# Weights and products of three attention stages by output tile, with PSUM banks owned by the phase

## The chip, the cores and the metric

The kernel runs on one core of a Trainium2 chip. A core has five engines, each with its own queue of instructions: PE (TensorE) multiplies matrices and writes the results to PSUM, DVE (VectorE) and ACT (ScalarE) work on tiles in SBUF and PSUM, POOL (GpSimd) works on SBUF, and SP issues most of the DMAs. PSUM has eight banks; one bank holds 512 fp32 numbers in each of 128 partitions. The metric is the time of one execution on the device, in microseconds (us), the median of several.

## The reference

One inference step of two layers over 288 tokens: 256 of a prompt and 32 of a sample group that has a cache of 256 past tokens. The model width is 1024, attention heads have 64 channels, the MLP is 4096 wide.

```
layer 0:  qa, ka, va, qb, kb, vb, fl = split(rmsnorm(x) @ ab_w_in)   # 8 heads A, 8 heads B
          A: attention over a band of chunks, relative bias, q and k normalised per head
          B: softmax attention with a forgetting term from log_sigmoid(fl + b)
          x += concat(A, B) @ ab_w_out
layer 1:  q, k, v = split(rmsnorm(x) @ sb_w_in)                      # 16 heads C
          C: stick-breaking attention
          x += C @ sb_w_out
each:     k_mem, v_mem = split(rmsnorm(mem) @ w_kv);  k_mem normalised
          x += cross_attention(rmsnorm(x) @ w_q, k_mem, v_mem) @ w_o  # 4 heads of 256
          x += square(relu(rmsnorm(x) @ w_up)) @ w_down
```

All is float32. The outputs are also the new keys and values of A, B, C, the memory keys and values, and log f.

## The kernel before

Everything is kept transposed: channels on the 128 partitions, the 288 tokens (`T`) along the free axis. The state `h` is 8 k-tiles of 128x288. A float32 product is made from three matmuls in a rounded format (`mm3`, lines 147 to 151): each operand is split into a high and a low part, and high times high, high times low and low times high are added in PSUM. So every weight is loaded by DMA into a raw buffer, rounded by ACT to `wh` (line 133; some by DVE, line 131), and subtracted by DVE to `wl` (line 134; in some stages by POOL).

Weights come in chunks of 256 output columns, two output tiles of 128. `load_chunk` (line 109) takes a chunk in two halves of four k-tiles, 512 KB each; four raw halves fit (`WR`), and three split halves (`WS // NQ`). The products of a chunk, 8 k-tiles x 2 output tiles x 3 = 48 matmuls, go to two PSUM banks, filled alternately by k (`gemm2` line 162, `Mix.products` line 498).

**Banks.** Two PSUM pools are opened once, at the top of `body`: `ps_g` with three banks for such products, and `ps_t` with one bank for nearly all else: transposes of values (`ps_vt`, line 402), sums of squares of heads (`ps_hn`, line 554), of memory keys (`ps_xn`) and of the memory (`ps_ms`), scores of the sample group (`ss` line 650, `zs` line 773), turned probabilities (`ps_pts`, `ps_ws`), and, in the phases ab and c, the sums of the RMS norm (`ps_rs`, line 203). Beside them each phase has a pool `s` of its own, in ab and c two buffers of two banks (`zz`, prompt scores). In x0 and x1 it has two single banks, and there are the pools `m` and `o` with one bank each.

**Phases.** `phase(kind)` (line 72) closes the last phase's pools, in SBUF and PSUM, and opens the next. There are four: ab (A, B and their output projection), x0 (cross-attention and MLP of layer 0), c (C and its output projection), x1 (the rest). At each border `norm_split` of the next part stands before the call of `phase`:

```
out_proj(i["ab_wo"], oh, ol)
xh, xl, rs = norm_split(1, 0)
phase("x0")
oh, ol = cross(0, xh, xl, rs, mk0, mh, ml)
```

**Order of the work.** A scheduler orders each engine's instructions by readiness and program order; `with ahead(n)` raises the priority of what it encloses. In the stages A, B and C, PE's order is written by hand (`manual_schedule`). A generator (`run_ab`, `run_c`) yields pieces of projection work, counted in matmuls: the q, k and v chunks of each group of four heads, the forget gate F, the memory M, N and the memory keys K. The attention code (`attend_ab`, `attend_c`) calls `fill(n)` at places where PE would otherwise wait for a softmax, and n matmuls' worth of projection is put there (`FILL_AB`, `FILL_C`). What has to follow a projection after some delay on PE (`norm_head`, `turn_v`, `mem_k_norm`) is put on a list by `later(n, fn)`; `due` runs what has come due, all at once.

**Evacuation.** When both tiles of a chunk are done, DVE reads the two banks: `t` for q and k of A and B (line 567), `vT` for values (line 530), `tmk` for memory keys (line 544), `qz` and `kT` in C (lines 724, 730), the addition to `h` in `out_proj` (line 841) and in the MLP (line 965). For q and k of A and B, ACT and DVE then form the two parts of the squares, PE sums them per head into `ps_hn` (lines 351, 352), ACT reads that bank and forms the root (`rstd_of`, lines 172 and 173), and DVE writes the normalised `qz` or `kT` (line 558).

## Time and profile before

| | |
|---|---|
| runs, us | 953.79, 955.01, 954.6; median 954.6 |
| profiled execution, us | 954.6 |
| its span, first to last instruction, us | 952.9 |
| granted TensorE clock, mean | 0.999 |
| DMA moved, MB | 160.01 |

By stretches of the span, from the table of windows (us of busy time):

| stretch | what runs | PE | DVE | ACT |
|---|---|---|---|---|
| 0 to 24 | load of `x`, first projections | 20.45 | 19.22 | 14.36 |
| 24 to 169 | stages A and B with projections and memory keys | 135.89 | 113.25 | 105.51 |
| 169 to 194 | `out_proj` of layer 0, start of cross-attention | 24.92 | 21.35 | 14.43 |
| 194 to 286 | cross-attention 0 | 92.00 | 70.66 | 49.50 |
| 286 to 491 | MLP 0, start of C's projections | 205.00 | 149.74 | 107.33 |
| 491 to 657 | stage C and its `out_proj` | 165.54 | 116.35 | 96.62 |
| 657 to 750 | cross-attention 1 | 92.51 | 76.20 | 47.98 |
| 750 to 953 | MLP 1 | 199.33 | 110.40 | 94.92 |

How to read the lines that follow. A line of a group names the source line, the engine, the operation, the tile written and the tiles read, the shapes, the count; behind the bar the busy time, the mean of one in ns, and the idle time before them with what ended it. A line of the waits names who waited, the releaser, and the total, the number of times and the longest wait in us. A line of the timeline has the start in us, the duration, and in brackets the engine's idle time before it. A line of the windows has the stretch, its length, the busy time and number of instructions of PE, its weight loads, DVE, ACT and POOL, the granted clock, the DMA share and GB/s. Matmuls overlap: one shows about 0.29 us, though they start 0.13 us apart.

### The profile page before, as it was taken

To read this page: it belongs to the slowest core of one execution; us is meant where nothing else is said; L and a number is where in the kernel's file an instruction comes from. 1 tells how busy PE (TensorE), PEld (TensorE's weight loads), DVE (VectorE), ACT (ScalarE), POOL (GpSimd) and SP (SyncE) were. 2 spreads that over 40 slices of the span, in tenths; PEclk is the share of its full clock that TensorE was granted. 3 is DMA by queue.
4 is the path that set the end of the run, shared out by engine and by line. 5 is a ranking of instruction groups with operands and counts; after the bars stand their busy time and mean duration, and the time that the engine had idled before them with its cause. 6 is when DMAs were issued, how large, how long until landed. Compare 5 with 4: busy or idle time off the path is not lost.

```text
span 952.9 us, 19195 instructions
## 1 busy us (share of the span) xinstructions
PE 935.6 (98%) x7284; PEld 909.1 (95%) x7284; DVE 677.2 (71%) x1462; ACT 530.7 (56%) x1232; POOL 161.2 (17%) x192
## 2 busy tenths in 40 slices
PE   8999899999999999999999999999999999999998
PEld 7889889999999999999999899999989999999998
DVE  8869858778687767676786757778977765555643
ACT  5868757556456635354556655654544665454531
POOL 4000000111122221122100000004434111111110
PEclk9999999999999999999999999999999999999999
DMA  7665444654554545554465444465444555545452
GB/s 240 237 201 164 153 159 161 219 174 156 166 167 157 175 157 170 162 173 161 158 205 183 146 158 136 158 221 172 148 134 145 162 171 165 167 161 171 155 177 73
DMA packets 50700, 160.01 MB, mean 168 GB/s; under 512 B 6296, under 2 KB 12968, under 8 KB 50352
## 3 DMA queue, kind: packets, MB, share of 16 engines
q1 hardware_dynamic: 46864, 148.69, 48.8%
q0 software_dynamic: 2592, 8.92, 2.4%
q10 hardware_dynamic: 1152, 1.18, 0.4%
q8 instruction: 57, 0.93, 0.4%
q14 instruction: 35, 0.29, 0.1%
HBM read 148.65 MB, written 10.12 MB: 167 GB/s over the span
## 4 chain that ended last, share of the span: by engine, by line
PE 87%; DVE 7%; ACT 3%; DMA 2%; issue 1%; SPq 0%; DVEq 0%; ACTq 0%
PE g L149 26%; PE g L150 26%; PE g L151 26%; DVE wl L134 2%; DMA raw<-in_ab_w_dram 1%; ACT wh L133 1%; PE zz L442 1%; DVE pr L664 1%; PE zz L813 1%; PE zz L768 1%; PE zz L452 1%; ACT pr L668 1%; DMA h<-in_xT_dram 0%; DVE spl L801 0%; PE sx L149 0%
## 5 line engine op out<-in xcount | busy, mean ns | idle before, releaser
L133 ACT ACTIVATE wh<-raw 128x512 fp32r<-128x512 f32 (+3 forms) x541 | 268.9, 547 | 245.6 <-PE g L150 130.8
L134 DVE TENSOR_TENSOR wl<-raw,wh 128x512 fp32r<-128x512 f32 (+3 forms) x519 | 318.0, 651 | 102.9 <-ACT wh L133 93.2
L149 PE MATMUL g<-xh,wh 128*128 128x288 f32 (+1 forms) x1032 | 304.2, 299 | 0.6 <-DVE tmk L544 0.3
L150 PE MATMUL g<-xl,wh 128*128 128x288 f32 (+1 forms) x1032 | 302.7, 296 | 1.2 <-DVE xl L186 1.1
L151 PE MATMUL g<-xh,wl 128*128 128x288 f32 (+1 forms) x1032 | 301.4, 296 | 1.3 <-DVE wl L134 1.3
L134 POOL TENSOR_TENSOR wl<-raw,wh 128x256 fp32r<-128x256 f32 (+2 forms) x105 | 123.1, 1172 | 435.0 <-ACT wh L133 331.8
L149 PEld LDWEIGHTS g<-xh,wh 128*128 128x128 f32 (+1 forms) x1032 | 191.8, 187 | 3.5 <-issue 0.9
L151 PEld LDWEIGHTS g<-xh,wl 128*128 128x128 f32 (+1 forms) x1032 | 192.2, 187 | 3.0 <-DVE wl L134 2.2
L150 PEld LDWEIGHTS g<-xl,wh 128*128 128x128 f32 (+1 forms) x1032 | 192.4, 187 | 2.7 <-DVE xl L186 2.2
L150 PE MATMUL g<-hl,wh 128*128 128x288 f32 x512 | 150.3, 295 | 0.0
L149 PE MATMUL g<-hh,wh 128*128 128x288 f32 x512 | 148.9, 295 | 0.0
L151 PE MATMUL g<-hh,wl 128*128 128x288 f32 x512 | 148.5, 294 | 0.0
L150 PEld LDWEIGHTS g<-hl,wh 128*128 128x128 f32 x512 | 96.1, 188 | 0.0
L151 PEld LDWEIGHTS g<-hh,wl 128*128 128x128 f32 x512 | 95.7, 188 | 0.0
L149 PEld LDWEIGHTS g<-hh,wh 128*128 128x128 f32 x512 | 95.3, 187 | 0.0
L150 PE MATMUL g<-ol,wh 128*128 128x288 f32 x256 | 75.1, 296 | 0.0
L149 PE MATMUL g<-oh,wh 128*128 128x288 f32 x256 | 74.0, 296 | 0.3 <-ACT oh L461 0.3
L151 PE MATMUL g<-oh,wl 128*128 128x288 f32 x256 | 73.7, 295 | 0.0
L131 DVE CAST wh<-raw 128x256 fp32r<-128x256 f32 (+2 forms) x83 | 32.5, 391 | 39.5 <-PE g L150 20.1
L965 DVE TENSOR_TENSOR h<-h,g 128x288 f32<-128x288 f32 x64 | 28.8, 451 | 29.6 <-PE g L151 29.5
L150 PEld LDWEIGHTS g<-ol,wh 128*128 128x128 f32 x256 | 48.1, 188 | 0.3 <-issue 0.2
L149 PEld LDWEIGHTS g<-oh,wh 128*128 128x128 f32 x256 | 47.5, 188 | 0.6 <-ACT oh L461 0.4
(272 smaller groups left out, 1418.3 us busy)
## 6 DMA issues: line engine op xcount, KB each, us to landing
raw<-in_w_up_dram SPq DMA_DIRECT2D x64, 512.0 KB, 3.8
raw<-in_w_down_dram SPq DMA_DIRECT2D x64, 512.0 KB, 3.8
raw<-in_w_kv_dram SPq DMA_DIRECT2D x32, 512.0 KB, 3.8
raw<-in_sb_w_dram SPq DMA_DIRECT2D x24, 512.0 KB, 4.2
raw<-in_ab_w_dram SPq DMA_DIRECT2D x22, 512.0 KB, 5.2
raw<-in_w_q_dram SPq DMA_DIRECT2D x16, 512.0 KB, 4.1
raw<-in_w_o_dram SPq DMA_DIRECT2D x16, 512.0 KB, 4.1
raw<-in_ab_wo_dram SPq DMA_DIRECT2D x8, 512.0 KB, 3.9
```

What stands on the lines that cost most here:

```text
L131: dve.tensor_copy(wh[:, r, :], src)
L133: cast = act(wh[:, r, :], src, AF.Copy).ins
L134: e.tensor_tensor(wl[:, r, :], src, wh[:, r, :].bitcast(F32), ALU.subtract)
L149: mm(out, lh, rh, start=first, stop=False)
L150: mm(out, lh, rl, start=False, stop=False)
L151: return mm(out, ll, rh, start=False, stop=last)
L442: mm(po[64 * par:64 * par + 64, kk * P:NP_], vt[:, kk, cols], pts[par][kk], start=kk == 0, stop=kk == 1)
L452: mm(po[64 * par:64 * par + 64, p * NS:(p + 1) * NS], vs[kk][:, cols], pts[kk][:, q], start=kk == 0 and p == 0, stop=kk == 2, skip_group_c ...
L664: dve.tensor_tensor_reduce(out=pr, in0=s, in1=b, scale=1.0, scalar=-3.0e38, op0=ALU.add, op1=ALU.max, accum_out=mx[:, j:j + 1])
L668: act(pr, pr, AF.Exp, bias=nm[:, j:j + 1], accum_out=sm[:, j:j + 1])
L768: mm(block(zz, e, kk), kT[r, p, kk * P:(kk + 1) * P], qz[r, p, kk * P:NP_].rearrange("p (b c) -> p b c", c=P), start=kk == 0, stop=False, ...
L965: dve.tensor_tensor(h[:, kt, :], h[:, kt, :], ps[:, 0:T], ALU.add)
```

## The change

**By output tile.** In A, B, C, their memory keys and their two output projections, a chunk is now worked one output tile of 128 columns after the other: 24 matmuls into one bank, then 24 into the next. `load_tiles` takes the place of `load_chunk` there: it loads the two raw halves, then splits the weights of the first tile from both halves, then those of the second; a buffer of split weights now holds all eight k-tiles of one output tile. `products` calls `take(d, ...)`, the evacuation, as soon as tile d is done, and yields 6 at a time. The first projection `qA0` keeps its old weights, sliced by tile.

**Banks.** The pools `ps_g` and `ps_t` are gone; each phase opens `g` and `t`: two banks each in ab and c, three and one in x0 and x1. The products of `kA0`, and of k of group 0 in C, go to a spare pair of `zz` banks.

**Order.** `due` counts all entries down and runs at most one per step. The delays become 36 for `norm_head` (were 30 and 42) and 24 for `turn_v` (were 18 and 36). `FILL_AB` gets a fifth entry, a fill behind the second pair's transposes. The evacuations of q, k and memory keys, and ACT's root in `norm_head`, get a raised priority.

```
-FILL_AB = 72, 30, 30, 12
+FILL_AB = 72, 24, 12, 24, 12
...
-    ps_g = ctx.enter_context(tc.tile_pool(name="ps_g", bufs=3, space=PS))
-    ps_t = ctx.enter_context(tc.tile_pool(name="ps_t", bufs=1, space=PS))
...
+        two = kind[0] != "x"
+        R.g = R.stack.enter_context(tc.tile_pool(name="g_" + kind, bufs=2 if two else 3, space=PS))
+        R.t = R.m = R.stack.enter_context(tc.tile_pool(name="t_" + kind, bufs=2 if two else 1, space=PS))
         R.s = R.stack.enter_context(tc.tile_pool(name="s_" + kind, bufs=2, space=PS))
-        R.m = ps_t
...
+    def load_tiles(ap):
+        raws = []
+        for half in range(2):
+            raws.append(wraw.tile([P, 4, CW], F32, tag="raw", name="raw"))
+            nc.sync.dma_start(out=raws[-1], in_=ap[:, half * 4:half * 4 + 4, :])
+        ws = []
+        for d in range(2):
+            wh = wspl.tile([P, KT, P], F32R, tag="wh", name="wh")
+            wl = wspl.tile([P, KT, P], F32R, tag="wl", name="wl")
+            for half in range(2):
+                r, src = slice(half * 4, half * 4 + 4), raws[half][:, :, d * P:(d + 1) * P]
+                R.count += 1
+                if R.dve_every and R.count % R.dve_every == 0:
+                    dve.tensor_copy(wh[:, r, :], src)
+                else:
+                    R.cast = act(wh[:, r, :], src, AF.Copy).ins
+                dve.tensor_tensor(wl[:, r, :], src, wh[:, r, :].bitcast(F32), ALU.subtract)
+            ws.append([(wh[:, k, :], wl[:, k, :]) for k in range(KT)])
+        towed()
+        return ws
...
         def due(self, n):
-            late, self.late = self.late, []
-            for at, fn in late:
-                if at > n:
-                    self.late.append([at - n, fn])
-                else:
-                    fn()
+            now = None
+            for item in self.late:
+                item[0] -= n
+                if now is None and item[0] <= 0:
+                    now = item
+            if now is not None:
+                self.late.remove(now)
+                now[1]()
...
-        def products(self, ap, xh, xl, n=T, ws=None, one_by_one=False):
+        def products(self, ap, xh, xl, take, n=T, ws=None, ps=None):
             if ws is None:
-                ws = load_chunk(ap)
...
+                ws = load_tiles(ap)
+            for d in range(2):
+                out = bank(R.g, "g") if ps is None else ps[d]
+                for k in range(KT):
+                    wh, wl = ws[d][k]
+                    mm3(out[:, 0:n], wh, wl, xh[:, k, 0:n], xl[:, k, 0:n], k == 0, k == KT - 1)
+                    if k % 2:
+                        if k == KT - 1:
+                            take(d, out[:, 0:n])
+                        yield 6
...
             r = scr.tile([P, T], F32, tag="f", bufs=FB, name="r")
-            rstd_of(ps[:, 0:T], T, 1.0 / 64, r)
+            with ahead(400):
+                rstd_of(ps[:, 0:T], T, 1.0 / 64, r)
...
-            if p == 0:
-                fill(FILL_AB[1])
+            fill(FILL_AB[1 + p])
...
+    def spare():
+        zz = R.s.tile([P, 2, 512], F32, tag="zz", name="zz")
+        return [zz[:, d, :] for d in range(2)]
...
-    def out_proj(wap, oh, ol):
+    def out_proj(wap, oh, ol, one_by_one=False):
         for n in range(4):
-            ws = load_chunk(wap[n])
-            pss = gemm2(ws, oh, ol)
+            if one_by_one:
+                ws = load_tiles(wap[n])
+                pss = []
+                for d in range(2):
+                    pss.append(bank(R.g, "g"))
+                    gemm([(pss[d][:, 0:T], slice(0, P))], ws[d], oh, ol, steps=())
+            else:
+                pss = gemm2(load_chunk(wap[n]), oh, ol)
```

More of the change, by code (lines that the diff above doesn't have):

```diff
@@ L101, in body @@
     nc.gpsimd.memset(epsb, EPS)
-    warm = bank(ps_t, "warm")
+    warm = bank(R.t, "warm")
     for _ in range(NWARM):
@@ L162, in gemm2 @@
     def gemm2(ws, xh, xl, n=T, steps=GO):
-        ps = [bank(ps_g, "g") for _ in range(2)]
+        ps = [bank(R.g, "g") for _ in range(2)]
         gemm([(ps[d][:, 0:n], slice(d * P, d * P + P)) for d in range(2)], ws, xh, xl, n, steps)
@@ L384, in mem_v @@
         v_ = R.ph.tile([P, 2, NP_], F32, tag="mv", name="mv", bufs=2)
-        pss = [bank(ps_g, "g") for _ in range(2)]
+        pss = [bank(R.g, "g") for _ in range(2)]
         for k0, k1 in zip((0,) + GO, GO + (KT,)):
@@ L401, in turn_v @@
     def turn_v(vT, vt, p):
-        pt = bank(ps_t, "ps_vt")
+        pt = bank(R.t, "ps_vt")
         for j in range(2):
@@ L527, in values @@
             nc.gpsimd.memset(vt[:, 2, :], 0.0)
-            yield from self.products(ap, xh, xl)
-            for p in range(2):
-                dve.tensor_tensor(vT[:, p, :], self.ps[p][:, 0:T], rs, ALU.mult)
-            nc.gpsimd.dma_start(out=out[:, 2 * g:2 * g + 2, :], in_=vT)
             def turn(p):
@@ L563, in qk, with take @@
             out = R.ph.tile([P, 2, T], F32, tag=tag, name=tag, bufs=QZB)
-            yield from mix.products(ap, xh, xl, **kw)
-            for p in range(2):
+            def take(p, ps):
                 t = R.ph.tile([P, T], F32, tag="tn", bufs=4, name="t")
-                last = dve.tensor_tensor(t, mix.ps[p][:, 0:T], rs, ALU.mult).ins
                 with ahead(400):
+                    last = dve.tensor_tensor(t, ps, rs, ALU.mult).ins
                     parts = square_parts(t)
-                mix.later(FILL_HN[p], lambda p=p, t=t, parts=parts: norm_head(p, t, parts, gain, out,
-                                                                             (lambda: then(out)) if p else None))
-            if tag == "kT" and mix.bias:
-                mix.bias.pop(min(mix.bias))(last)
+                mix.later(36, lambda: norm_head(p, t, parts, gain, out, (lambda: then(out)) if p else None))
+                if p and tag == "kT" and mix.bias:
+                    mix.bias.pop(min(mix.bias))(last)
+            yield from mix.products(ap, xh, xl, take, **kw)
         for step in steps:
@@ L649, in attend_ab @@
             pairs.append((zz, pr))
-        sp = bank(ps_t, "ss")
+        sp = bank(R.t, "ss")
         for p in range(2):
@@ L694, in attend_ab @@
             pts.append(pt)
-            if p == 0:
-                fill(FILL_AB[1])
-        pp = bank(ps_t, "ps_pts")
+            fill(FILL_AB[1 + p])
+        pp = bank(R.t, "ps_pts")
         for kk in range(3):
@@ L701, in attend_ab @@
         act(pt, pp[:, 0:3 * P], AF.Copy)
-        fill(FILL_AB[2])
+        fill(FILL_AB[3])
         vt = vt()
@@ L707, in attend_ab @@
             put_prompt(oh, ol, kt0 + p, zz[:, 0, :])
-        fill(FILL_AB[3])
+        fill(FILL_AB[4])
         po = pairs[1][0][:, 1, :]
@@ L721, in run_c, with take @@
                 qz = R.ph.tile([P, 2, T], F32, tag="qz", name="qz", bufs=QZB)
[L722 to L724 removed]
+                def take(p, ps, qz=qz):
+                    dve.scalar_tensor_tensor(qz[:, p, :], ps, 0.125, rs, ALU.mult, ALU.mult)
+                yield from mix.products(i["sb_w"][g], xh, xl, take)
                 mix.done["q", g] = qz
@@ L727, in run_c, with take @@
                 kT = R.ph.tile([P, 2, T], F32, tag="kT", name="kT", bufs=KTB)
-                yield from mix.products(i["sb_w"][4 + g], xh, xl, one_by_one=g == 0)
-                for p in range(2):
-                    dve.tensor_tensor(kT[:, p, :], mix.ps[p][:, 0:T], rs, ALU.mult)
+                def take(p, ps, kT=kT):
+                    dve.tensor_tensor(kT[:, p, :], ps, rs, ALU.mult)
+                yield from mix.products(i["sb_w"][4 + g], xh, xl, take, ps=spare() if g == 0 else None)
                 nc.gpsimd.dma_start(out=o["ckT"][:, 2 * g:2 * g + 2, :], in_=kT)
@@ L772, in attend_c @@
             zzs.append(zz)
-        zp = bank(ps_t, "zs")
+        zp = bank(R.t, "zs")
         for p in range(2):
@@ L817, in attend_c @@
             wps.append(w)
-        pp = bank(ps_t, "ps_ws")
+        pp = bank(R.t, "ps_ws")
         for kk in range(3):
@@ L1009, in turn @@
         def turn():
-            ps = bank(ps_t, "ps_cq")
+            ps = bank(R.t, "ps_cq")
             for j in range(2):
```

68 lines of the change are left out of this document (28 added, 40 removed).

## The prediction

> **What bounds the kernel now.** I read the page first, then TensorE's waits, then the table of stretches, then the timeline at the borders between phases.
>
> ```profile
> span 952.9 us, 19195 instructions
> PE 935.6 (98%) x7284; PEld 909.1 (95%) x7284; DVE 677.2 (71%) x1462; ACT 530.7 (56%) x1232; POOL 161.2 (17%) x192
> PEclk9999999999999999999999999999999999999999
> ```
>
> The execution took 954.6 us, 1.7 more than its span; the median of the three runs is 954.6 too, so the sum below needs no shift. TensorE (PE) is busy 98% at full clock: any saving must be PE standing still for less time. Nothing here removes a matmul.
>
> ```profile
> PE ps_hn L351 <- ACT r L172: 2.4, 2, 2.0
> PE g L149 <- DVE tmk L544: 1.3, 2, 1.0
> ...
> PE ps_ms L325 <- ACT r L172: 1.2, 1, 1.2
> ...
> PE ps_pts L699 <- ACT r L172: 1.1, 1, 1.1
> ...
> PE ps_hn L351 <- ACT cq L1013: 1.0, 1, 1.0
> PE ps_vt L404 <- DVE mx L664: 0.6, 2, 0.3
> PE ps_hn L352 <- DVE sl L346: 0.6, 1, 0.6
> PE ps_pts L699 <- ACT vt L407: 0.6, 1, 0.6
> ...
> PE g L149 <- DVE t L567: 0.2, 1, 0.2
> ```
>
> These are PE's waits in stages A, B and C (total, times, longest). In all rows but one PE is about to write a PSUM bank, and the releaser is the instruction that read the bank's previous tile: `ps_hn` waits for the ACT that reads the `ps_hn` before it. These are waits for banks. The one bank of `ps_t` costs 2.4 + 1.2 + 1.1 + 1.0 + 0.6 + 0.6 = 6.9 us in 8 waits, the three of `ps_g` 1.3 + 0.2 = 1.5 in 3. The seventh row (`sl`) is a wait for data. A wait also costs more than its row:
>
> ```profile
> 286.00:491.00 205.00, 205.00 (x1541) 204.90 (x1540) 149.74 (x361) 107.33 (x296) 39.47 (x48) 1.00 0.53 169
> ...
> 111.11 0.29 PE L151 MATMUL g<-xh,wl 128*128 128x288 f32 x1
> 113.38 0.40 PE L351 MATMUL ps_hn<-sh,bdr 128*128 128x288 f32 x1 [1.98 <-ACT r L172]
> ```
>
> In the MLP of layer 0 (286 to 491) PE issues one matmul each 205/1541 = 0.133 us. At the longest wait, starts lie 2.27 us apart, 2.14 more than that pace, where the row says 1.98. With 0.16 for each of 11 waits the bank waits cost 8.4 + 1.8 = 10.2 us.
>
> **What the change takes away.** With two `t` banks, a tile has until the next but one to be read. With tiles one after the other, a `g` bank has the 24 matmuls of the other tile, 24 × 0.133 = 3.2 us, to be read in; now the next chunk wants a second bank 3 matmuls (0.4 us) after the pair ended. So nearly all 11 waits lose their cause. What is late next is VectorE:
>
> ```profile
> 84.00:96.00 12.00, 10.91 (x84) 10.42 (x84) 11.19 (x25) 11.12 (x29) 1.13 (x3) 1.00 0.47 143
> 96.00:108.00 12.00, 11.72 (x117) 10.43 (x114) 9.73 (x34) 7.92 (x24) 0.44 (x2) 1.00 0.60 203
> 108.00:120.00 12.00, 9.44 (x70) 8.97 (x69) 11.70 (x36) 10.08 (x33) 0.00 (x0) 1.00 0.30 91
> 120.00:132.00 12.00, 10.21 (x83) 9.66 (x82) 5.65 (x11) 8.09 (x21) 1.08 (x2) 1.00 0.65 211
> ```
>
> (Columns: PE, weight loads, DVE, ACT, POOL.) From 84 to 120 DVE works 32.6 of 36 us while PE idles 3.9; without these 3.9 PE would want 32.6 us of DVE work in 32.1. Only weights split ahead (three tiles, 9.6 us of PE) and the slack after 120 can lend that. So the gain lies between 4 (these waits come back as waits for `wl` and at other places) and 10.2; I take three quarters, **7.5**, as half of the idle time lies where DVE has room. Half of the `sl` wait, **0.3**, goes through the raised priority of the evacuations. `FILL_AB` sums to 144 before and after; the one-a-step `due` only spreads work: 0.
>
> The Trainium skill speaks against the banks: "TensorE: Matmul & The Clock Gate", section "HAM oscillation — how this bites in real kernels", reports a kernel in which PSUM double-buffering gave no further gain. That kernel waited for DMA; the rows above name bank readers, so the trace does not agree; by it the 7.5 would be 0 and the sum 964.8.
>
> **What it moves.** Weights: a chunk still takes 4 casts and 4 subtractions of 128x512, and two DMAs on SP's queue; so do the memory keys and the two `out_proj`. But both raw halves are held until the second tile is split, so a refill is asked for later.
>
> ```profile
> raw<-in_ab_w_dram SPq DMA_DIRECT2D x22, 512.0 KB, 5.2
> ...
> ACT wh L133 <- DMA raw<-in_ab_w_dram: 4.4, 4, 1.9
> ```
>
> A half takes 5.2 us to land and ACT waited 4.4 us in all for such data, with hardly any of it reaching PE. The later request is bounded by 0 and by those 4 waits of up to 1.9 (7.6); I take **+0.3**, near 0, since three tiles of PE (9.6 us), less the splitting, lie between request and use.
>
> At the start, `qA0` by tile would put up to 21 matmuls (2.8 us) behind the last arriving k if the order were kept.
>
> ```profile
> 7.96 0.43 PE L149 MATMUL g<-xh,wh 128*128 128x288 f32 x2
> ```
>
> There the program writes L149, L150, L151 of one tile and then the other's; the trace has L149 twice: outside the hand-ordered part, PE's order is made by readiness. So I take 0 (0 to +2.8; −0.5 if it falls better).
>
> **What it adds: a hand-over at each border of phases.** Before, `ps_g` and `ps_t` lived throughout. Now they belong to the phase, and each phase's pools fill all eight banks (2 + 2 + 4; 3 + 1 + 2 + 1 + 1), so a new `g` lies on old banks. How memory passes from an old pool to a new one, the trace shows in SBUF:
>
> ```profile
> 168.35 0.41 PE L452 MATMUL zz<-pts,vt 128*64 128x32 f32 x8
> 168.90 0.33 SPq L850 DMA_DIRECT2D cmv<-in_cmv_dram  x1
> ...
> SPq L850 <- PE zz L452: 4.8, 2, 4.2
> ```
>
> `cmv`, the first transfer into phase x0's pool, stood in SP's queue up to 4.2 us and was issued 0.14 us after the last matmul that reads phase ab's pool. By order of first use `cmv` lies on that pool's `bmask`, `qz` and `tn`, read long before; `vt` and `pts` come later in it. At x1 it is the same (2 times). So a new pool waits for the last reader of all old pools beneath it. For `g` at x0 the last reader is not `out_proj`'s evacuation: `norm_split` stands before `phase("x0")`, and its `ps_rs` lies in `t`.
>
> ```profile
> 187.51 0.29 PE L151 MATMUL g<-oh,wl 128*128 128x288 f32 x1
> 187.64 0.30 PE L149 MATMUL g<-xh,wh 128*128 128x288 f32 x1
> ...
> 190.39 0.44 DVE L841 TENSOR_TENSOR h<-h,g 128x288 f32<-128x288 f32 x1
> 190.86 0.54 ACT L185 ACTIVATE xh<-h,gT 128x288 fp32r<-128x288 f32 x1 [3.26 <-DVE h L841]
> 191.31 0.43 ACT L200 ACTIVATE sq<-h 128x288 f32<-128x288 f32 x1
> 192.32 0.45 DVE L202 TENSOR_TENSOR ssum<-ssum,sq 128x288 f32<-128x288 f32 x1
> 194.02 0.65 PE L205 MATMUL ps_rs<-ssum,ones 128*128 128x288 f32 x2
> 195.23 0.48 ACT L172 ACTIVATE rs<-ps_rs,epsb 128x288 f32<-128x288 f32 x1
> ```
>
> Today PE goes from the last `oh` product straight to `xh` products, and these hide the chain below them. Then they could start only after L172. All later PE work of the phase stands behind them in its queue, so the cover is gone. The chain at its shortest is 0.44 + 0.54 + 0.43 + 0.45 + 0.65 + 0.48 = 3.0, with six passings of 0.05 **3.3 us**; at its longest it is today's 187.80 to 195.71, 7.9. Border c to x1 is alike:
>
> ```profile
> 650.16 0.29 PE L151 MATMUL g<-oh,wl 128*128 128x288 f32 x1
> 650.29 0.30 PE L149 MATMUL g<-xh,wh 128*128 128x288 f32 x1
> ...
> 656.70 0.50 ACT L172 ACTIVATE rs<-ps_rs,epsb 128x288 f32<-128x288 f32 x1 [1.69 <-PE ps_rs L205]
> ```
>
> Its longest is 650.45 to 657.20, 6.8. With PE standing, fewer splits compete on DVE and ACT, but some, already started, do (the addition at 190.39 came 2.6 us after its product): I take 3.3 + 1.1 = **4.4** each, nearer the short end. At m0 to c the rms reads a bank of its own; only `g`'s last evacuation counts:
>
> ```profile
> 484.68 0.29 PE L151 MATMUL g<-hh,wl 128*128 128x288 f32 x1
> 484.81 0.30 PE L149 MATMUL g<-xh,wh 128*128 128x288 f32 x1
> ...
> 486.11 0.45 DVE L965 TENSOR_TENSOR h<-h,g 128x288 f32<-128x288 f32 x1
> ...
> 493.02 0.48 ACT L172 ACTIVATE rs<-ps_rs,epsb 128x288 f32<-128x288 f32 x1
> ```
>
> 0.55 (0.45 and a passing of 0.1) to 1.6 (484.97 to 486.56); I take **1.1**. C's first k goes to spare banks that lie on those of x0's `ps_rs`: 48 matmuls (6.4 us) after 486.1 it would find L172 done at 493.5, 0 to 1.0 late; I take 0.3. In all 2 × 4.4 + 1.1 + 0.3 = **10.2** (2 × 3.3 + 0.55 = 7.2 to 7.9 + 6.8 + 1.6 + 1.0 = 17.3).
>
> **Sum.** 954.6 − 7.5 − 0.3 + 0.3 + 10.2 = **957.3 us**.
>
> **Rivals.**
> - *The hand-over costs nothing* (the other side): banks pass on tile by tile. It decides if `g`'s first bank, read 3.2 us before `out_proj` ends, is free by itself. Against it: the `cmv` rows. 954.6 − 7.5 = 947.1. 14%.
> - *Short hand-overs, all waits gone*: 3.3 twice, 0.55, 0.3 for the spare; 10.2 and all 0.6 of `sl` saved: 954.6 − 10.8 + 7.5 = 951.3. For: L841 comes first on DVE in program order. Against: DVE's stretches. 12%.
> - *DVE takes the banks' place* in B: only 4 gained, 954.6 − 4 + 10.5 = 961.1. For: 11.7 of 12 us. The rule on double-buffering from the Trainium skill, above, goes the same way and further. 16%.
> - *The clock falls* in the two long gaps: if PE then ran at half rate for as long as it stood (4.4, my choice), each costs 2.2 more: 957.3 + 4.4 = 961.7. Against: the stretch 108 to 120, with its wait of 2.0, is granted 1.00; no gap of before is longer. The Trainium skill, same page, section "What's actually happening", has the clock halved after an idle window of about 3.4 us and back after a busy one; no run here shows it; by it an estimate is 1.7 each, 960.7. 8%.
>
> **Numbers.** The forecast holds 50%, with its own range 953 to 962 (hand-overs 8 to 13, gain 5 to 9.5). 0.2%, 1.9 us, is about what a measurement of this kernel can tell from no change: 952.7 to 956.5. Slower: 0.34 + 0.14 + 0.08 = 0.56; same: 0.15 + 0.01 + 0.02 + 0.04 = 0.22; faster: 0.01 + 0.13 + 0.08 = 0.22. The range 949.5 to 963.5 leaves out most of the first rival (0.12) and 0.06 above.
>
> **What would show it.** In the profile after: PE waits at `g` L149 for ACT `rs` L172 (or with `ps_rs` just before), two of 3 to 6 us, at the ends of both `out_proj`; one near 1 us for DVE `h` L965 ahead of C; no wait of `ps_hn`, `ps_ms`, `ps_pts` for L172, L407 or L1013. I am wrong if `xh` products of x0 start before L172 has read `ps_rs`, or if new `wl` or `raw` waits in B exceed 3 us.

## The result, and the profile after

The changed kernel is slower: 977.9 us (median of 4 runs, 977.6 to 979.8) against 954.7 (4 runs, 953.8 to 955.0), a ratio of 1.0245 with a 95% interval of 1.0232 to 1.0257. The forecast was 957.3, with a range of 949.5 to 963.5: the sign was right and the size was not; 20.6 us are missing from the sum. The profiled execution of the changed kernel was its longest, 979.8 us, so the stages below add up to 25.1 us more than before, where the medians give 23.2.

The page of the changed kernel, its first lines (columns as before):

```profile
span 978.1 us, 19162 instructions
PE 943.9 (97%) x7284; PEld 918.3 (94%) x7284; DVE 679.2 (69%) x1462; ACT 530.6 (54%) x1232; POOL 159.0 (16%) x192
PEclk9999899989999999999999999999999999999999
```

The number of TensorE's instructions is unchanged, yet PE is busy 8.3 us longer, and the clock row has an 8 in two slices where it had none. So there are two losses to look for: PE standing still, and PE running slowly. The table of stretches separates them. The borders are the starts of A/B with its output projection, the cross stage x0, the MLP of layer 0, C with its projection, and x1 (the MLP of layer 1 behind it is unchanged: 208.4 and 208.5 us); the columns are the length, PE's busy time with its matmuls, the granted clock, and two on DMA. First the kernel before:

```profile
0.00:187.80 187.80, 175.06 (x1396) 1.00 0.60 194
187.80:280.10 92.30, 92.30 (x737) 1.00 0.49 160
280.10:485.00 204.90, 204.90 (x1540) 1.00 0.53 167
485.00:650.40 165.40, 164.94 (x1347) 1.00 0.52 171
650.40:744.40 94.00, 93.51 (x737) 1.00 0.46 147
```

and the changed kernel, each hand-over counted to the stage behind it:

```profile
0.00:194.10 194.10, 179.45 (x1394) 0.97 0.57 188
194.10:295.50 101.40, 95.33 (x737) 0.97 0.45 146
295.50:500.40 204.90, 204.90 (x1539) 1.00 0.52 167
500.40:670.30 169.90, 165.16 (x1347) 1.00 0.49 166
670.30:769.50 99.20, 94.06 (x737) 0.98 0.43 140
```

Length less busy time is what PE stood still:

| stage | longer by | PE stood: before, after | PE busy longer by |
|---|---|---|---|
| A/B and projection | 6.3 | 12.7, 14.7 | 4.4 |
| x0 | 9.1 | 0.0, 6.1 | 3.0 |
| MLP 0 | 0 | 0, 0 | 0 |
| C and projection | 4.5 | 0.5, 4.7 | 0.2 |
| x1 | 5.2 | 0.5, 5.1 | 0.6 |
| sum | 25.1 | +16.9 | +8.2 |

I had expected nearly all of the 7.5 us in A/B, where all but 0.3 us of the bank waits lay. A/B got 6.3 longer, and that is the largest error. PE's waits say what happened there (total, times, longest):

```profile
PE ps_rs L230 <- DVE ssum L227: 7.4, 2, 3.9
PE ps_hn L376 <- ACT sh L369: 4.9, 3, 2.2
PE g L174 <- DVE h L1001: 2.5, 1, 2.5
PE zz L174 <- DVE t L591: 2.4, 1, 2.4
PE ps_xn L376 <- DVE sh L359: 2.1, 1, 2.1
PE ps_hn L377 <- DVE sl L371: 1.5, 4, 0.6
...
PE g L174 <- ACT rs L197: 1.2, 2, 0.6
```

Every bank wait that I had listed is gone: no `ps_hn`, `ps_ms` or `ps_pts` waits for the reader of a bank. The waits for weights that I had named as a sign of being wrong did not grow (`wl` 0.6 us in all, 1.3 before). In place of the bank waits stand waits for data, the squares `sh` and `sl` (4.9 + 2.1 + 1.5 = 8.5 us), and one at a score tile `zz` (2.4). At the borders it is as forecast: `ps_rs` waits for the sum of squares, then the first product of the cross stage for `rs`. The border into x0, in the timeline:

```profile
193.85 0.29 PE L176 MATMUL g<-oh,wl 128*128 128x288 f32 x1
198.07 1.33 PE L230 MATMUL ps_rs<-ssum,ones 128*128 128x288 f32 x2 [3.93 <-DVE ssum L227]
200.00 0.61 PE L174 MATMUL g<-xh,wh 128*128 128x288 f32 x1 [0.59 <-ACT rs L197]
200.40 0.44 PE L175 MATMUL g<-xl,wh 128*128 128x288 f32 x1
200.64 0.44 PE L176 MATMUL g<-xh,wl 128*128 128x288 f32 x1
```

The last product of the projection starts at 193.85 and the first of x0 at 200.00, 6.15 us later, where before they were 0.13 apart: a shift of 6.0 (I had 4.4). The next products come 0.24 us apart, not 0.13. The table of stretches around the two falls of the clock in A/B:

```profile
27.10:30.50 3.40, 3.40 (x15) 0.50 0.93 300
...
112.40:119.20 6.80, 6.35 (x26) 0.50 0.41 144
```

In A/B, 15 matmuls take 3.40 us and 26 take 6.35; at 0.133 us each they would take 2.0 and 3.5. That is 4.3 us, the whole 4.4 by which PE is busy longer there.

### The profile page after: what moved, and what is told of

It is laid out like the page before. It is cut to its first block, busy times and chain, and to the rows that moved or that the text cites. A ratio compares the mean times of both kernels' runs of the same rounds, so it can differ in the third digit from the quotient of the medians.

```text
span 978.1 us, 19162 instructions
## 1 busy us (share of the span) xinstructions
PE 943.9 (97%) x7284; PEld 918.3 (94%) x7284; DVE 679.2 (69%) x1462; ACT 530.6 (54%) x1232; POOL 159.0 (16%) x192
## 3 DMA queue, kind: packets, MB, share of 16 engines
q10 hardware_dynamic: 1152, 1.18, 0.4%
## 5 line engine op out<-in xcount | busy, mean ns | idle before, releaser
L174 PE MATMUL g<-xh,wh 128*128 128x288 f32 (+1 forms) x1000 | 299.9, 304 | 3.9 <-DVE h L1001 2.5
L175 PE MATMUL g<-xl,wh 128*128 128x288 f32 (+1 forms) x1000 | 297.0, 299 | 1.2 <-DVE xl L211 1.1
L133 ACT ACTIVATE wh<-raw 128x256 fp32r<-128x256 f32 (+2 forms) x405 | 190.2, 522 | 196.9 <-PE g L175 98.5
L176 PE MATMUL g<-xh,wl 128*128 128x288 f32 (+1 forms) x1000 | 295.5, 299 | 0.6 <-DVE wl L134 0.6
L134 DVE TENSOR_TENSOR wl<-raw,wh 128x256 fp32r<-128x256 f32 (+2 forms) x363 | 220.8, 645 | 89.7 <-ACT wh L133 85.2
L174 PEld LDWEIGHTS g<-xh,wh 128*128 128x128 f32 (+1 forms) x1000 | 189.5, 191 | 7.7 <-ACT wh L155 2.7
L175 PEld LDWEIGHTS g<-xl,wh 128*128 128x128 f32 (+1 forms) x1000 | 189.9, 191 | 2.4 <-DVE xl L211 2.0
L176 PEld LDWEIGHTS g<-xh,wl 128*128 128x128 f32 (+1 forms) x1000 | 189.6, 191 | 2.0 <-DVE wl L134 1.4
L175 PE MATMUL g<-hl,wh 128*128 128x288 f32 x512 | 150.5, 295 | 0.0
L156 DVE TENSOR_TENSOR wl<-raw,wh 128x512 fp32r<-128x512 f32 x156 | 101.5, 684 | 6.6 <-ACT wh L155 5.3
L155 ACT ACTIVATE wh<-raw 128x512 fp32r<-128x512 f32 x136 | 79.4, 622 | 45.0 <-PE g L175 29.7
```

The lines of the kernel that those rows point to most:

```text
L133: cast = act(wh[:, r, :], src, AF.Copy).ins
L134: e.tensor_tensor(wl[:, r, :], src, wh[:, r, :].bitcast(F32), ALU.subtract)
L155: R.cast = act(wh[:, r, :], src, AF.Copy).ins
L156: dve.tensor_tensor(wl[:, r, :], src, wh[:, r, :].bitcast(F32), ALU.subtract)
L174: mm(out, lh, rh, start=first, stop=False)
L175: mm(out, lh, rl, start=False, stop=False)
```

## The experiments

Each kernel was run beside the kernel before on the same chip, and ratios are to that. `Theory 1` is about the borders and `Theory 2` about A/B.

### The borders, and two guesses at A/B

**e1_tilewait** lets each tile of a PSUM pool wait for its own bank only:

```diff
-        R.g = R.stack.enter_context(tc.tile_pool(name="g_" + kind, bufs=2 if two else 3, space=PS))
+        R.g = R.stack.enter_context(tc.tile_pool(name="g_" + kind, bufs=2 if two else 3, space=PS, reuse_waits="tile"))
...
```

> The changed kernel with one word more: each of the five PSUM pools made per phase lets a tile wait only for the earlier users of its own bank, not for every user of the pools released before it. Theory 1 (the hand-over by whole pools is what stands at the three phase borders, and the half clock behind the first of them comes from that gap): the shifts of +6.0, +2.7 and +5.0 us at the borders go, and with them the 3.4 us lost at the half clock at 197.7 to 204.6 us: 977.9 - 13.7 - 3.4 = about 961 us, the A/B stage as it is. Rival (the gaps at the borders are the data of the norm, the chain from the last add to h over the squares to the reciprocal root, which comes late because the output tiles end late): the borders keep at least three quarters of their shifts, 973 us or more.

Measured 977.0 us (ratio 1.0242, 1.0224 to 1.0260): not to be told from the changed kernel, against my theory. TensorE's instructions stand in exactly the order of the changed kernel, with `ps_rs` ahead of the first products of x0 and x1; PE still waits 7.3 us for `ssum` at `ps_rs`. Only the last layer of the border is gone: the first products no longer wait for `rs`, and the borders into x0 and x1 are 4.9 and 4.3 us, not 6.1 and 5.1.

**e2_before_pools** is the kernel before with pools per phase:

```diff
-    ps_g = ctx.enter_context(tc.tile_pool(name="ps_g", bufs=3, space=PS))
-    ps_t = ctx.enter_context(tc.tile_pool(name="ps_t", bufs=1, space=PS))
...
+        R.g = R.stack.enter_context(tc.tile_pool(name="g_" + kind, bufs=3, space=PS))
+        R.t = R.m = R.stack.enter_context(tc.tile_pool(name="t_" + kind, bufs=1, space=PS))
```

> The kernel before with nothing of the change but the pools of g and t made anew in each phase, in their old sizes (3 banks and 1), so that tiles, orders and delays are those of before. Theory 1 (hand-over by whole pools): the three borders come up as in the changed kernel, +13.7 us, and +3.4 us for a half clock behind the first gap: 968 to 972 us. Rival (the borders are late data of the tile-by-tile order): within 2 us of before, under 957 us.

Measured 968.0 (1.0142, 1.0127 to 1.0158): pools per phase alone cost 13.5 us, with nothing done tile by tile. The border into x0 in its timeline:

```profile
187.87 0.29 PE L150 MATMUL g<-oh,wl 128*128 128x288 f32 x1
191.30 0.37 PE L148 MATMUL g<-xh,wh 128*128 128x288 f32 x1 [3.13 <-DVE h L840]
```

A/B ends at 187.87, as before (187.51). The border is 3.4 us, not 6.15, and PE waits for the last addition to `h`, not for the norm: here three `g` banks lie on three `g` banks, and the bank of `ps_rs` is under none of them; in the trace `ps_rs` comes at 197.28, behind the first products. So a border of the changed kernel has two layers, the wait for the last evacuation and the norm on top of it.

**e3_spare2** puts the two output tiles that go to a spare score tile into two:

```diff
-        zz = R.s.tile([P, 2, 512], F32, tag="zz", name="zz")
-        return [zz[:, d, :] for d in range(2)]
+        return [R.s.tile([P, 2, 512], F32, tag="zz", name="zz")[:, 0, :] for d in range(2)]
```

> The changed kernel with the two output tiles of kA0 and of C's k0 in two separate score tiles, not in the two halves of one. Theory 1 (the second output tile waits for the reading of the first because both lie in one tile): the waits of 2.4 us at 24.2 and of 0.8 us at 513.0 go, and the half clock of 27.1 to 30.5 us (1.7 us lost) goes if the gap of 24.2 us fed it: 973 to 975.5 us. Rival (the data behind it is late anyway, so the wait moves to the next matmul on it): no gain, 977 us or more.

Measured 977.2 (1.0235, 1.0219 to 1.0250), not to be told from the changed kernel. The wait of `zz` for `t` is gone and `out_proj` ends 2.3 us earlier in its profile; but its clock falls at other places (21.68, 110.43 and 147.97 us in A/B). That this hides so small a difference is likely, not shown. The edit comes up again below.

**e4_later** asks for the norms later:

```diff
-                mix.later(36, lambda: norm_head(p, t, parts, gain, out, (lambda: then(out)) if p else None))
+                mix.later(60, lambda: norm_head(p, t, parts, gain, out, (lambda: then(out)) if p else None))
...
-                    self.later(48, lambda: self.done.update({key: mem_k_norm(layer, g, t, parts)}))
+                    self.later(72, lambda: self.done.update({key: mem_k_norm(layer, g, t, parts)}))
```

> The changed kernel with the work that follows a q or k tile put later: norm of a head after 60 units of other matmuls, not 36, and of a memory key after 72, not 48. Theory 1 (in the A/B stage the bank waits were traded for waits for squares that are not ready after 36 units): the waits of ps_hn and ps_xn for sh and sl, 8.5 us in all on the page of waits, mostly go, and with them 3.4 us at the half clock of 112.4 to 119.2 us: 966 to 971 us. Rival (VectorE and ScalarE are late as a whole, delays only move where TensorE waits): 975 us or more.

Measured 974.9 (1.0211, 1.0194 to 1.0228), 3.0 us less than the changed kernel, between the two and at the rival's edge. The longest of its new waits:

```profile
PE g L174 <- DVE tmk L564: 3.5, 1, 3.5
PE ps_vt L429 <- DVE vT L553: 2.2, 1, 2.2
PE ps_pts L722 <- ACT r L197: 1.5, 1, 1.5
```

The waits for squares are gone from the list; these three are new, and one of 1.2 us of `ps_hn` for `vt`. The second is for the values `vT`, whose turning I had not put later. The third and the one for `vt` are waits for a reader of a bank: with other delays they come up with two banks as well.

### The borders closed, and the banks by themselves

**e6_persist** keeps two banks for output tiles and one for the small products over all phases; one more is handed over:

```diff
+    ps_g = ctx.enter_context(tc.tile_pool(name="ps_g", bufs=2, space=PS))
+    ps_t = ctx.enter_context(tc.tile_pool(name="ps_t", bufs=1, space=PS))
...
+        ps_e = R.stack.enter_context(tc.tile_pool(name="e_" + kind, bufs=1, space=PS))
+        R.g = ps_g if two else Turns(ps_e, ps_g, ps_g)
+        R.t = R.m = Turns(ps_t, ps_e) if two else ps_t
...
-            ps = bank(R.m, "ps_rs")
+            ps = bank(ps_t, "ps_rs")
```

`Turns` takes its pools in turn.

> The changed kernel with the same number of banks for each use in each phase, but two banks for output tiles and one for the small products are kept over all phases, and only one more bank is handed over (second of the small products in A, B, C and the MLP; third of the output tiles in the cross phases, where it is taken first). Theory 1, as it stands after the first four runs (the third bank of a cross phase lies on a bank of the small products, so the sum of the norm, ps_rs, was put ahead of the first products of the phase on TensorE's queue, and letting each tile wait for its own bank did not undo that order): the first products stand ahead of ps_rs again and the borders go back to at most 1 us each: 977.9 - 12 to 13.7 - 3.4 at the half clock = 961 to 963 us, the A/B stage as it is. Rival (the data of the norm is late because the output tiles end one by one): 973 us or more.

Measured 962.2 (1.0068, 1.0053 to 1.0083), 15.7 us less, as theory 1 said. The border into x0:

```profile
194.47 0.29 PE L187 MATMUL g<-oh,wl 128*128 128x288 f32 x1
194.61 0.30 PE L187 MATMUL g<-xh,wl 128*128 128x288 f32 x1
```

It is 0.14 us, and the other two are 0.14 and 0.13. A/B is as long as in the changed kernel (it ends at 194.47): borders and A/B are two separate losses. `ps_rs` stands behind the first products again, and these cover the norm's chain; that the chain ends late is no loss as long as nothing stands behind it.

**e7_oldbanks** has the tile order and the banks of before:

```diff
-        R.g = R.stack.enter_context(tc.tile_pool(name="g_" + kind, bufs=2 if two else 3, space=PS))
-        R.t = R.m = R.stack.enter_context(tc.tile_pool(name="t_" + kind, bufs=2 if two else 1, space=PS))
+        R.g, R.t, R.m = ps_g, ps_t, ps_t
```

> The changed kernel, tile by tile, with the banks of before: three for output tiles and one for the small products, kept over all phases. No border has a hand-over, so beside the run with persistent pools it gives what the second bank of the small products is worth once the work goes tile by tile. Theory 1 (the bank waits of before stood over waits for squares and products that VectorE and ScalarE deliver late, so freeing the bank frees little): within 2 us of that run, 960 to 965 us. Rival (the second bank takes some 8 to 10 us of waits away, and the delays of 36 and 48 units alone brought others): 968 us or more.

Measured 967.6 (1.0125, 1.0108 to 1.0142). Against e6_persist, where one of the three `g` banks is a second small bank, that bank is worth 5.4 us: neither side had it right. And the tile order with all that goes with it (delays, fills, spare score tiles), with the banks of before and no border, costs 12 us.

```profile
PE ps_hn L377 <- ACT sh L370: 4.8, 3, 2.1
PE ps_pts L723 <- ACT r L198: 2.8, 3, 1.8
```

The bank wait of `ps_pts` is back, beside the waits for squares.

**e8_chunkw** splits the weights by rows as before, and the tiles take halves of these pieces:

```diff
-                ws = load_tiles(ap)
+                ws = by_tile(load_chunk(ap))
```

> The changed kernel with the weights split by rows of a chunk, as before, and the output tiles read as halves of those pieces; order, banks and delays as changed. Theory 1 (the order of the split and the longer held raw buffers cost little): within 2 us, 976 to 980 us. Rival (raw buffers that are held over both tiles hold the loads back and make the first piece of a weight late): 974 us or less, most of it in the A/B stage.

Measured 980.2 (1.0264, 1.0244 to 1.0284): not faster, rather 2.3 us slower. That raw buffers are held longer is not what costs.

**e9_warmgap** fills two gaps:

```diff
+    wg = bank(R.t, "wg")
+    for _ in range(16):
+        mm(wg[:, 0:P], ones, h[:, 6, 0:P], start=True, stop=True)
     xh, xl, rs = norm_split(1, 0)
```

> The changed kernel with 16 more products of 128x128 on TensorE in the gap of each of the two borders to a cross phase, ahead of ps_rs and on data that is there (h of the last output tile but one); nothing uses them. Theory 1 (the clock halves because TensorE stood still): the gap stays, x0 starts as late as before at +12 us, but the granted clock stays at 1 behind it and the first products go at 0.13 us each, not 0.24: 3 to 3.6 us less, 974 to 975 us. Rival (the half clock does not hang on the gap): the granted clock of 0.5 comes at the same place for 6.8 us, 977.5 us or more.

Measured 973.7 (1.0192, 1.0177 to 1.0207), 4.2 us less. The same 7 us behind the border into x0, first in the changed kernel, then in this one (all engines: PE, weight loads, DVE, ACT, POOL, clock, DMA):

```profile
197.70:204.60 6.90, 5.93 (x21) 5.11 (x22) 0.32 (x1) 0.94 (x2) 0.00 (x0) 0.51 0.24 77
```

```profile
198.00:205.00 7.00, 7.00 (x54) 7.00 (x54) 2.05 (x3) 2.33 (x4) 0.00 (x0) 1.00 0.13 39
```

From the end of `out_proj` to x0's first product it still takes 5.6 us (6.15 in the changed kernel), but then 54 matmuls run where 21 did. No fall of the clock comes behind either border. Useless work in a gap is what kept it up; what the fall costs is about 2 us behind the border into x0 (19 products at 0.24 instead of 0.13) and about 0.6 behind that into x1, less than the 4.2: in this execution A/B was also 1.8 shorter, with other waits and falls of the clock of its own.

### A/B: score tiles and follow-up

**e10_persist_spare2** is e6_persist with the two spare score tiles of e3_spare2.

> The kernel with banks kept over all phases (962.2 us, e6_persist), and the two output tiles of kA0 and of C's k0 in two separate score tiles. Theory 2 (the waits at 24.3 and in C come from two tiles in the halves of one): 2.6 + 1.2 us of waits go and 1.7 us at the half clock of 27.6: 956.5 to 959 us. Rival (VectorE's data are late there anyway): 961 us or more.

Measured 958.2 (1.0031, 1.0020 to 1.0043): 4.0 us less. In its profile the waits of 2.6 and 1.2 us are gone, and so is the fall of the clock at 27.57 us, right behind the first of them. The edit that couldn't be told from nothing by itself is worth about its waits and that fall here. Its worth isn't fixed: with the shared score tile the same wait for `t` is 0.7 us in the profile of e9_warmgap and 2.9 in that of e1_tilewait.

**e11_distances** puts the follow-up of a weight where before had it in the sequence. The changed kernel counts from the end of each tile; before counted from the end of the pair, and gave the second tile 12 and 18 units more than the first:

```diff
-                mix.later(36, lambda: norm_head(p, t, parts, gain, out, (lambda: then(out)) if p else None))
+                mix.later((60, 48)[p], lambda: norm_head(p, t, parts, gain, out, (lambda: then(out)) if p else None))
...
-                self.later(24, lambda: turn(p))
+                self.later((48, 42)[p], lambda: turn(p))
...
-                    self.later(48, lambda: self.done.update({key: mem_k_norm(layer, g, t, parts)}))
+                    self.later(54, lambda: self.done.update({key: mem_k_norm(layer, g, t, parts)}))
```

(The step that sets a delay counts 6 units of its own, so 60 is 54 after the tile.)

> The kernel of e10_persist_spare2, and the follow-up of each weight put back to its place in the sequence of before: norm of the first tile 54 units after the tile's end and of the second 42 (the changed kernel: 30 and 30), turning of v 42 and 36 (18 and 18), norm of a memory key 48 (42). Theory 2 (the A/B stage lost 6.4 us because the follow-up now comes sooner after the end of its tile than VectorE and ScalarE can deliver): the waits for sh and sl of 18.9, 80, 110 and 148 us, 8.6 us in all, mostly go, with the half clock of 112.9 us: 3 to 8 us under e10_persist_spare2, 950 to 955 us. Rival (these two engines are late as a whole, and the wait moves to the next thing they owe): within 2 us of e10_persist_spare2.

Measured 951.8 (0.9973, 0.9961 to 0.9984): 6.4 us less, and now faster than before. All waits for `sh` are gone; one long one is left. The chain of it, in the timeline, from ScalarE and VectorE:

```profile
143.14 0.47 ACT L208 ACTIVATE rx<-ps_xn,epsb 128x256 f32<-128x256 f32 x1
...
147.72 0.63 ACT L166 ACTIVATE wh<-raw 128x512 fp32r<-128x512 f32 x1 [2.65 <-DMA raw<-in_ab_wo_dram]
148.25 0.40 ACT L209 ACTIVATE rx<-rx 128x256 f32<-128x256 f32 x1
...
148.99 0.87 DVE L407 SCALAR_TENSOR_TENSOR mk<-tmk,xqkg,rx 128x256 f32<-128x256 f32 x2
...
149.90 0.76 DVE L575 TENSOR_TENSOR tmk<-g,memrs 128x256 f32<-128x256 f32 x2
```

PE stands 5.7 us, to 150.5, for a `g` bank that `tmk` has not read. VectorE is not busy: `tmk` has no buffer, because the norm of an earlier memory key is unfinished. The first step of its `rx` ran at 143.14, the second only at 148.25; between them on ScalarE's queue stands a weight piece that waits 2.65 us for its load.

**e12_distances_oldbanks** is the same with the banks of before (and the spare score tiles).

> Tile by tile with the banks of before (967.6 us, e7_oldbanks), with the separate score tiles and the follow-up at the places of before. Theory 2 (the tile order itself costs nothing, its earlier follow-up and the shared score tile do): within 3 us of before, 952 to 958 us. Rival (the tile order costs by itself, with one bank for the small products): 960 us or more.

Measured 961.2 (1.0066, 1.0054 to 1.0079), on the rival's side. With the follow-up in place the second small bank is worth 961.2 − 951.8 = 9.4 us. Without it, the tile order is still 6.2 us slower than the kernel before. Its waits are for banks again, and longer than those of before:

```profile
PE ps_hn L377 <- ACT r L198: 3.7, 2, 3.2
PE ps_pts L723 <- ACT rx L198: 3.1, 1, 3.1
PE ps_pts L723 <- ACT r L198: 2.8, 1, 2.8
```

**e13_phasefirst** makes the pools ahead of the norm:

```diff
-    xh, xl, rs = norm_split(1, 0)
-    phase("x0")
+    phase("x0")
+    xh, xl, rs = norm_split(1, 0)
```

> The changed kernel with the pools of a cross phase made ahead of the norm in front of it, so that the sum of the norm, ps_rs, takes a bank of the new phase and stands behind the phase's first products on TensorE's queue. Theory 1 (one border is made of the wait for the last add to h, some 3.3 us as with pools alone in e2_before_pools, and of ps_rs ahead of the first products, the rest): the shifts of 6.0 and 5.0 us fall to 3.3 each, m0 to c stays at 2.7: about 4 us less, 972.5 to 975 us. Rival (the whole border is the pool, whatever stands ahead): no gain, 977 us or more.

Measured 970.1 (1.0162, 1.0147 to 1.0178): 7.8 us less than the changed kernel, more than the 4 expected. `ps_rs` now stands behind the first products:

```profile
193.38 0.29 PE L176 MATMUL g<-oh,wl 128*128 128x288 f32 x1
195.76 0.37 PE L174 MATMUL g<-xh,wh 128*128 128x288 f32 x1 [2.09 <-DVE h L877]
```

The borders are 2.4, 1.9 and 1.6 us, the first 3.8 us shorter than in the changed kernel, and the clock doesn't fall behind any of them.

### What was still open

**e14_t2three** gives the tag of `tmk` (which it shares with `vT` and a few others) a third buffer, and takes two scratch tiles for the room:

```diff
-FB = 8
+FB = 6
...
-            t = scr.tile([P, 2, T], F32, tag="t2", name="tmk")
+            t = scr.tile([P, 2, T], F32, tag="t2", bufs=3, name="tmk")
```

> The kernel of e11_distances (951.8 us) with three buffers, not two, for the tile that holds a memory key (and six, not eight, of the small scratch tiles, for the room). Theory 2 (the one long wait left in A/B, 5.7 us for tmk at 144.5 us, is for a buffer: the third memory key can't be written before the first one's norm has read it): the wait falls under 2 us and the half clock behind it goes: 945 to 949 us. Rival (VectorE is late there whatever it has to write to, or fewer scratch tiles cost as much): 951 us or more.

Measured **947.1 us** (0.9916, 0.9902 to 0.9929): the fastest kernel of the study, 0.8% faster than before. The longest waits that PE has left:

```profile
PE ps_hn L388 <- DVE sl L382: 1.7, 2, 1.2
PE ps_hn L387 <- ACT r L208: 1.3, 2, 0.7
```

The wait for `tmk` is gone, and after the start the clock no longer falls. A/B with its projection ends at 181.68, 5.8 us before the kernel before.

**e16_dist_only** is the changed kernel with the follow-up of e11_distances alone.

> The changed kernel with nothing but the follow-up of each weight at the places of before (54 and 42 units for norms, 42 and 36 for v, 48 for memory keys). Theory 2: the gain that it brought beside the other edits, 6.4 us, comes alone too: 970 to 973 us, with the borders as in the changed kernel. Rival (it pays only once the score tiles are apart): 975 us or more.

Measured 972.7 (1.0183, 1.0167 to 1.0199): 5.2 us less. It doesn't need the other edits. All waits for `sh` are gone here too, and the wait for `tmk`, 5.1 us, has come in their place.

**e17_mkahead** puts the norm of a memory key ahead instead of giving it room:

```diff
-        xnorm_from(parts, t, NP_, xqkg[:, layer, 1, :], k_)
+        with ahead(400):
+            xnorm_from(parts, t, NP_, xqkg[:, layer, 1, :], k_)
```

> The kernel of e11_distances (951.8 us) with the norm of a memory key put ahead on ScalarE and VectorE, as the changed kernel does with the norm of a head, so that its tile is read and free sooner; buffers as they are. Theory 2 (the wait of 5.7 us for tmk is for its buffer, which the late second step of the norm holds, 4.7 us behind the first on ScalarE): the wait falls to 2 us or less: 946 to 949.5 us. Rival (VectorE is late as a whole): 951 us or more.

Measured 952.6 (0.9973, 0.9963 to 0.9983): nothing gained over e11_distances, and the wait for `tmk` is still 5.3 us. The second step of `rx` (146.40) still follows a weight piece that waits 2.3 us for its load. So the buffer is the cause, and priority was the wrong way to free it.

**e18_tile_phasefirst** joins e13_phasefirst and e1_tilewait.

> The changed kernel with the pools of a cross phase made ahead of the norm (970.1 us, e13_phasefirst), and each tile of a PSUM pool waiting for the earlier users of its own bank alone. In e13_phasefirst 2.4, 1.7 and 1.4 us are left at the borders. Theory 1a (what is left is the wait for every user of the pools before): they go, 964 to 966.5 us. Theory 1b (the first product's own bank is that of the last output tile, since with two banks both are in use to the end): they stay, 969 us or more.

Measured 968.3 (1.0134, 1.0120 to 1.0147). Both theories hold, each at its border. At x0 the wait stays (as between the MLP and C); at x1 it is gone:

```profile
192.01 0.29 PE L176 MATMUL g<-oh,wl 128*128 128x288 f32 x1
194.39 0.37 PE L174 MATMUL g<-xh,wh 128*128 128x288 f32 x1 [2.08 <-DVE h L877]
...
664.86 0.29 PE L176 MATMUL g<-oh,wl 128*128 128x288 f32 x1
665.00 0.30 PE L174 MATMUL g<-xh,wh 128*128 128x288 f32 x1
```

Phase ab has one more `g` tile than c, the 8 rows of the forget gates, so its last output tile lies in the bank that x0 takes first; in c it lies in the other. That reading follows from the count of tiles; it was not tried by itself. Why waits by tile left the order of `ps_rs` as it was (e1_tilewait) stays open.

## Why the prediction failed, step by step

The runs cut the way from before to after into parts, and on to the best version:

| step | us | from, to |
|---|---|---|
| tile order with its follow-up, banks of before | +12 | 955.5, 967.6 |
| second small bank | −5.4 | 967.6, 962.2 |
| borders, with the clock behind them (the change complete) | +15.7 | 962.2, 977.9 |
| from there: borders closed again | −15.7 | 977.9, 962.2 |
| score tiles apart | −4.0 | 962.2, 958.2 |
| follow-up at its old places | −6.4 | 958.2, 951.8 |
| a third buffer for `tmk` | −4.7 | 951.8, 947.1 |

(The kernel before measured 954.6 to 955.5 beside them, so the parts are good to about 1 us.)

- **What bounds the kernel**: right in kind. PE's standing made 16.9 of the 25.1 us; the other 8.2 are PE running slowly, for which my sum had no term. The rows named as bank waits were bank waits: in the changed kernel none of them is left, and with the banks of before (e12_distances_oldbanks) they come back.
- **The gain of 7.5**: the size of the mechanism is right, 5.4 us in the change as it is (e7 to e6) and 9.4 once the follow-up is in place (e12 to e11), inside my 4 to 10.2. But A/B didn't get it, and this is the step that failed. I wrote that `FILL_AB` sums to 144 and that the one-a-step `due` only spreads work, "0", and I didn't price the delays at all. The diff replaces 30 and 42 units from the end of the pair by 36 from the end of each tile, 6 of which the step that sets the delay counts itself. So the second tile has 12 units (1.6 us at 0.133) less between its last product and its norm, and the second tile of v 18 less to its turning. The norm of the first tile comes 24 units earlier than at its old place in the sequence. The squares were asked for before ScalarE and VectorE had made them: 8.5 us of waits, and half-clock stretches behind them. Undoing it gave 6.4 us beside the other edits and 5.2 alone.
- **Which tile waits**: all three waits of `ps_hn` for `sh` (4.9 us) are at the first tile of a pair, in qA0, qB0 and qB1. From the start of the evacuation `t` to the point at which PE wanted the sum there were 3.1, 5.0 and 7.8 us in the kernel before; in the changed kernel there are −0.7 (PE wanted it before the evacuation began), 2.6 and 3.4. To the end of `sh` it took 1.3, 3.2 and 1.3 us before, and 1.3, 3.2 and 5.5 after. So in the first two the engines were as quick as before and were asked sooner; in qB1 ScalarE was also later. This pair in the kernel before, first tile's evacuation and second tile's squares:

```profile
101.60 0.46 DVE L567 TENSOR_TENSOR t<-g,rs 128x288 f32<-128x288 f32 x1 [0.50 <-PE g L151]
105.75 0.45 DVE L346 TENSOR_TENSOR sl<-sqh,sh 128x288 fp32r<-128x288 f32 x1
```

  and its first tile in the changed kernel:

```profile
106.75 0.45 DVE L591 TENSOR_TENSOR t<-g,rs 128x288 f32<-128x288 f32 x1
109.84 0.29 PE L176 MATMUL g<-xh,wl 128*128 128x288 f32 x1
111.81 0.43 ACT L369 ACTIVATE sh<-t 128x288 fp32r<-128x288 f32 x1
112.29 0.53 PE L376 MATMUL ps_hn<-sh,bdr 128*128 128x288 f32 x1 [2.15 <-ACT sh L369]
```

  In the kernel before, the first norm of this pair started at 109.38 without a wait, and the wait of 1.98 us behind 111.11 was at the second, whose squares were done at 106.20: no wait for data lay under that bank wait. The wait at 109.84 is a new one, at the other tile.
- **Spare banks**: I priced only those of C, at 0.3. That both output tiles of kA0 lie in one score tile, so that the second waits for the reading of the first (2.4 us at 24.2, 0.8 in C), I didn't see: 4.0 us.
- **Squares `sl`, 0.3 gained**: wrong, 0.6 became 1.5 us. **Raw buffers, +0.3**: splitting by rows as before gained nothing (e8_chunkw). **Start, 0**: little loss there beyond the waits above: with these gone, the first score product comes at 36.5 in e11_distances and at 35.9 before.
- **Hand-overs, 10.2**: the mechanism was right at each border: `g` waits for `rs`, with `ps_rs` ahead of it, and the MLP's border only for `h`. But most of the border into x0 is the order on TensorE's queue and the late addition to `h`, not the wait of `g` itself: with waits by tile (e1_tilewait) 4.9 of the 6.1 us stay. The terms were too small: 6.0, 2.7 and 5.0 us, 13.7 where I had 4.4, 1.1 and 4.4. I took the chain near its shortest. At 193.85 VectorE was on other work that ended late: the last addition to `h` came at 195.65, 1.8 us after the last product had started, and the norm's chain behind it took until 200.0.
- **The clock**, a rival at 8%: it fell, behind both long borders, and in A/B where I had no gap at all. I argued from a wait of 2.0 that had left it alone. The falls in A/B and behind the border into x0 make up most of the 8.2 us by which PE is busy longer.
- **DVE in the banks' place**, at 16%: the new waits are in A/B, as it said, but a full VectorE is not their cause. With the follow-up put back, and VectorE's work as it was, they go, and the second small bank gives 9.4 us.
- **The hand-over for nothing** gave 947.1 in the forecast. The kernel with the borders closed and the three other losses undone is at 947.1. The agreement is partly luck, but it says that what the change is after was there.

## What to carry to other kernels

A delay that is counted in work is part of the schedule: when the point moves from which it is counted, work it out again for each user, from the end of the data to the use. Work out, for each operand, the time from its being ready to its use, before and after: for the first tile of qB1 it fell from 7.8 us behind the evacuation to 3.4, where the squares took 5.5. When a memory pool is made anew inside a pipeline, ask which old tile lies under its first bank and where that tile's reader stands in the queue; with one of the four banks for products handed over instead of all four, the kernel was 15.7 us faster here.

## What the runs showed of the clock

The clock fell after much shorter gaps than I thought. In the changed kernel it fell at 27.07, 112.41, 197.74 and 675.6 us, for 3.41 us or twice that; these times lie on one grid of 3.413 us (25, 25 and 140 steps apart). Such a grid can be laid over all 18 traces (before, after, the 16 experiments), and in each step at full clock the time summed in which no matmul ran. From 12 us on there are 4,941 steps at full clock. In 52 of them it was 1.84 us or more, and the next step ran at half clock each time; in the 4,889 others it was at most 1.85, and no next step did. At half clock, the next step was at full clock again if PE had stood 0.43 us or less, and stayed at half from 0.45 on. So in this kernel, behind its start, somewhat over half a step decides, and where a gap lies against the grid decides with it. In the first 12 us these limits don't hold: there the clock fell behind ten steps in which PE had stood only 1.0 to 1.7 us. Why is open. The gap at 109.84 in the changed kernel puts 2.15 us into one step and costs 3 us more; that at 148.24, no shorter, is cut by a line into 1.43 and less, and costs nothing; in e1_tilewait the grid lies otherwise, the gap at the same place puts 2.19 us into one step, and the clock falls. The wait of 1.98 at 111.11 in the kernel before, which I had taken as proof that 2 us are harmless, was cut as well: 1.18 us of it lie in one step. This makes parts under 2 us hard to measure in a kernel with such gaps, as probably in e3_spare2.

The Trainium skill, "TensorE: Matmul & The Clock Gate", section "What's actually happening", describes a free-running window of 3413 ns and says that the clock halves after an idle window and is back after a busy one; the traces agree with the window's length and that it runs freely. They don't agree with "idle" taken as wholly idle: behind the start, windows in which TensorE worked for up to 1.57 of 3.41 us halved the clock.
